# Hybrid attention and retention layer on one Trainium2 core: last gating on VectorE with its store on GpSimd's queue, retention's roots stored by one transfer, first product of attention's half 0 one step earlier

## The chip, the core and the metric

The kernel runs on one core of one Trainium2 chip. The core has a matmul engine (TensorE, PE in the profile, with its weight loads under PEld), three engines for elementwise work (VectorE = DVE, ScalarE = ACT, GpSimd = POOL) and SyncE (SP), which does nothing here but issue DMA transfers. Each engine takes its instructions in order; a transfer issued from a queue waits there until its operands are ready, and everything behind it on that queue waits with it. The metric is the device time of one execution in microseconds; less is better. Before the change three runs took 1901.03, 1903.34 and 1903.62 us, median 1903.34.

## What is computed

One layer on x of 2048 tokens by 1024 channels. The reference, cut to what matters:

```python
h = rms_norm(x, norm_gain)
q_a, k_a, v_a, g_a, q_r, k_r, v_r, g_r, m_a, m_r = split_columns(h @ w_in)
o_a = chunk_band_attention(q_a, k_a, v_a, rel_bias)      # 8 heads of 64, own chunk of 64 and 8 before
branch_a = (o_a * silu(g_a)) @ w_out_attn                # "gating" of attention
o_r = retention_chunkwise(rotary(q_r), rotary(k_r), v_r, gn_gain)   # 8 heads, keys 64, values 128
#   ... at its end: o = (o - mean) * rsqrt(var + GN_EPS), per head and token
branch_r = (o_r * silu(g_r)) @ w_out_ret
mixed = sigmoid(m_a) * branch_a + sigmoid(m_r) * branch_r
return rms_norm(x + mixed @ w_out, final_gain)
```

## The kernel before

**Dense stream.** All projections (`p0`, `g0`, `p1`, `g1`, then the two output projections `ba`, `br`, and `out`) are one long list of products of 128x128 by 128x512 tiles. Every fp32 operand is split in two parts (h and l), so that a product takes three matmuls (h by h, h by l, l by h); these three are one **dense step**, about 0.68 us of PE. Accumulators lie in PSUM (`ps_p_*`, `ps_g_*`, `ps_ba_*`), epilogues on DVE and ACT read them out, and results that a later part needs go through DRAM scratch.

**Phases.** The tokens are taken in two halves s = 0, 1. The order is proj0, attention of half 0 (att0), retention of half 0 (ret0), proj1, att1, ret1, and the merge (mrg). Dense steps are woven into the attention and retention phases by hand (`fill(n)` makes n dense steps). `later(n, fn)` emits fn n dense steps from now; `put(lag, dst, src)` is such a deferred store on SP's queue (`dma`, L154). `flush()`, at the end of a phase, emits what is still deferred. So the code itself sets the order on each engine; only in the merge may DVE, ACT and POOL be reordered by a scheduler.

**Tiles of a phase.** Each phase opens its own pool `E` of 128x512 tiles (11 buffers in attention, 12 in retention, L56 and L57). The pool of the next phase lies on the memory of the one before, and a tile waits for the last users of the memory that it lies on, so a load of the next phase may wait for a store of the phase before. In the built program the transfers of SP's and ACT's queues also share eight completion semaphores in rotation; a transfer that comes round to one still in use waits for its owner.

**Attention** (`attention`, from L1413). A unit is a head h and a block b of 512 tokens; a half has 16 units, b = 2s and 2s+1 for each head. Scores (`wide`) get bias and minimum on DVE, exponential on ACT, scaling on POOL (`pr`); PE transposes them in six groups (`tp`), ACT and DVE split each into `pth` and `ptl`, and `product` (L1547) multiplies them with the values into the PSUM tile `po`, which all units share. A group's product comes `PV_LAG` = 3 dense steps after its transposes, two more for group 0 (L1569). After group 5 `out_` (L1560) adds the two halves of `po` into `oa` (ACT copy, then DVE add), POOL multiplies `oa` by the gate `ua` three steps later, and SP stores it to DRAM scratch `oas` six steps after `out_`. The next phase begins with SP's loads of `kr` and `qr`, the keys and queries of the first retention step, for which PE waits to make the scores `sr`; POOL clears parts of `qr` first.

**Retention** (`retention`, from L1615). 4 pairs p of heads by 4 time steps of 256 tokens in each half. `sums` (L1790) adds the squares of row r = 4 (st - 4s) + p into the PSUM tile `ssq` with a one-hot weight. At the end of the phase a chain of 12 small DVE operations on 16 rows makes the inverse roots (`rt`, the tile `y`), and four stores of 8x1x256 put them into the scratch `rss`, laid out by block and head; chain and stores take one deferred step each, 16 in all, and as many dense steps go under them. The merge and the second pass read them back as `rb` (`finish_yr`, L1240).

**Behind the two retentions.** proj1 begins with four loads `b_p` of weight columns of its second chunk (L1956 and on): ACT casts them (`wh_p`), DVE forms the rests (`wl_p`, `t_p`). About the same time SP refills the resident operands `r` from scratch `cs`. The merge begins with loads of `raw_ba` (weights of `ba0`), `ga` (gates, read in by `before_ba`, used by the epilogue at L1275), `oas` and, for `finish_yr`, `yr`, `yv` and `rb`; DVE gates `yr` (L1248, L1251), ACT and DVE split it into `r` (L1257, L1258).

Of the kernel before, what the change touches and what calls it, by code (L numbers as in the profile page):

```python
# [16 lines left out]
ALU = mybir.AluOpType  # L17
# [4 lines left out]
P = 128  # L22
# [6 lines left out]
B = 512  # L29
# [31 lines left out]
PV_LAG = 3  # L61
# [12 lines left out]
def hybrid_kernel(  # L74
# [30 lines left out]
    def r32(ap):  # L105
        return ap.bitcast(F32)

    def ACC(name):
        return ps_acc.tile([P, 512], F32, tag="acc", name=name)
# [4 lines left out]
    def E(name, dt=F32, shape=(P, 512)):  # L114
        return epool[0].tile(list(shape), dt, tag="e", name=name)
# [4 lines left out]
    def D(name, shape, dt=F32):  # L120
        return dram.tile(list(shape), dt, name=name)

    def open_phase(name, e_bufs, tr_bufs=0):
        st = ExitStack()
        phase[0] = st
        epool[0] = st.enter_context(tc.tile_pool(name=f"e_{name}", bufs=e_bufs, reuse_waits="tile"))
        if tr_bufs:
            xpool[0] = st.enter_context(
                tc.tile_pool(name=f"tr_{name}", bufs=tr_bufs, space=PSUM, reuse_waits="tile")
            )  # L130
        return st
# [21 lines left out]
    pe, act, dve, pool = Ordered(nc.tensor), Sometimes(nc.scalar), Sometimes(nc.vector), Sometimes(nc.gpsimd)  # L153
    dma = Ordered(nc.sync).dma_start  # L154
# [27 lines left out]
    oascr = [[D(f"oas_{p}_{b}", [P, B]) for b in range(NB)] for p in range(4)]  # L182
# [7 lines left out]
    escr = D("escr", [HEADS, 511])  # L190
    bandscr = [D(f"band_{h}", [P, 256]) for h in range(HEADS)]
    stscr = [D(f"sts_{p}", [HD, 2 * DV]) for p in range(4)]
    rsscr = [D(f"rss_{s}", [16, B]) for s in range(2)]
    skscr = [D(f"sks_{p}", [P, 2 * DV], F32R) for p in range(4)]


# [48 lines left out]
    def later(n, fn):  # L245

        order[0] += 1
        deferred.append((steps[0] + n, order[0], fn, free[0]))
        deferred.sort(key=lambda e: e[:2])
# [8 lines left out]
    def put(lag, dst, src):  # L258

        later(lag, lambda: dma(dst, src))  # L260
# [979 lines left out]
    def finish_yr(h, b, m, lead, hold=0):  # L1240

        a, u, r = (E(f"{n}_{h}_{b}") for n in ("yr", "yv", "rb"))
        dma(a, orscr[h // 2][b][h % 2])
        dma(u, urscr[h][b])
        dma(r, rsscr[b // 2][8 * (b % 2) + h].rearrange("(o d) -> o d", o=1).broadcast_to([P, B]))

        def gated():
            dve.scalar_tensor_tensor(a, a, gn[:, h:h + 1], u, ALU.mult, ALU.mult)  # L1248

        later(lead, gated)  # L1250
        later(lead + 2, lambda: (pool if m is None else dve).tensor_tensor(a, a, r, ALU.mult))  # L1251
        if m is None:
            put(lead + 8, yrscr[h], a)
            return
        wh, wl = (w[:, h % 4, :] for w in R[m])
        at = max(lead + 5, hold - steps[0])
        later(at, lambda: act.copy(wh, a))  # L1257
        later(at + 2, lambda: dve.tensor_tensor(wl, a, r32(wh), ALU.subtract))  # L1258
# [154 lines left out]
    def attention(s, sbp, ps_wide):  # L1413
# [4 lines left out]
        units = [(h, b) for h in range(HEADS) for b in (2 * s, 2 * s + 1)]  # L1418
# [106 lines left out]
        def weighted(h, b, gr):  # L1525

            k0 = 0 if b > 0 else 4
            js = ((0, 1), (2,), (3,), (4,), (5,), (7, 6))[gr]
            tp = ACC(f"tp_{h}_{b}_{gr}")
            c, cut, parts = 0, [], []  # L1530
            for j in js:
                ts = range(max(0, j - 4), min(4, j + 1))
                cut.append((j, c, ts))
                for t in ts:
                    at = (j - max(t, k0)) * P
                    pe.transpose(tp[:, c:c + P], prs[h, b, t][:, at:at + P], ident)
                    c += P

            def part(which):
                p = E(f"pt{which}_{h}_{b}_{gr}", F32R)  # L1540
                parts.append(p)
                if which == "h":
                    act.copy(p[:, 0:c], tp[:, 0:c])
                else:
                    dve.tensor_tensor(p[:, 0:c], tp[:, 0:c], r32(parts[0][:, 0:c]), ALU.subtract)

            def product():  # L1547
                for j, at, ts in cut:
                    n = len(ts) * P
                    v4 = vts[h, b - 1 + j // 4][:, j % 4, :]  # L1550
                    for i, p in enumerate(parts):
                        pe.matmul(
                            po[:, ts[0] * P:ts[0] * P + n], v4, p[:, at:at + n],
                            start=j == (0 if b > 0 else 4) and i == 0, stop=gr == 5 and j == 6 and i == 1,
                            skip_group_check=True,
                        )
                if gr == 5:
                    later(1, out_)

            def out_():  # L1560
                oa, u = E(f"oa_{h}_{b}")[0:64], uts[h, b]
                act.copy(oa, po[64:128])
                later(1, lambda: dve.tensor_tensor(oa, po[0:64], oa, ALU.add))
                later(3, lambda: pool.tensor_tensor(oa, oa, u, ALU.mult))
                put(6, oascr[h // 2][b][64 * (h % 2):64 * (h % 2) + 64], oa)

            part("h")
            later(1, lambda: part("l"))
            later(PV_LAG + (2 if gr == 0 else 0), product)  # L1569

        def plan(b):

# [42 lines left out]
    def retention(s, ps_ret):  # L1615
# [8 lines left out]
        for n in range(3):  # L1624
            t = epool[0].tile([P, 2, 2, T], F32R, tag=f"q{n}", bufs=1, name=f"qr_{s}_{n}")
# [112 lines left out]
        def sure(here):  # L1738

            while not here():  # L1740
                emit()
# [18 lines left out]
        def evacuate(p, st, ops):  # L1760
            b, un = st // 2, st % 2
            nm = f"{p}_{st}"
            got = []

            def out_():
                oz = E(f"oz_{nm}")
                o2 = E(f"o2_{nm}")
                act.copy(oz, ops)
                act.activation(o2, ops, AF.Square)
                put(  # L1770
                    2,
                    orscr[p][b][:, :, un * T:(un + 1) * T].rearrange("i p t -> p i t"),
                    oz.rearrange("p (i t) -> p i t", i=2),
                )
                later(2, lambda: high(o2))

            def high(o2):
                got.append(E(f"o2h_{nm}", F32R))
                act.copy(got[0], o2)
                later(2, lambda: low(o2))  # L1780

            def low(o2):
                got.append(E(f"o2l_{nm}", F32R))
                pool.tensor_tensor(got[1], o2, r32(got[0]), ALU.subtract)

            later(1, out_)

            def sums():
                sure(lambda: len(got) == 2)
                r = 4 * (st - 4 * s) + p  # L1790
                for n, t in enumerate(got):
                    pe.matmul(
                        ssq, ohr[:, ONE - r:ONE - r + 16], t, start=not begun[0],
                        stop=(p == 3 and st == 4 * s + 3 and n == 1), skip_group_check=True,
                    )
                    begun[0] = True

            return sums
# [14 lines left out]
        for n, (p, st, i) in enumerate(items):  # L1813
# [24 lines left out]
        y, tmp, hv, var = (E(f"rt{n}")[0:16] for n in range(4))  # L1838
        chain = [
            lambda: dve.tensor_scalar(var, ssq, 1.0 / DV, GN_EPS, ALU.mult, ALU.add),  # L1840
            lambda: dve.tensor_scalar(tmp.bitcast(I32), var.bitcast(I32), 1, None, ALU.logical_shift_right),
            lambda: dve.tensor_scalar(y.bitcast(I32), tmp.bitcast(I32), -1.0, RSQRT_MAGIC, ALU.mult, ALU.add),
        ]
        for _ in range(3):
# [2 lines left out]
                lambda: dve.tensor_tensor(tmp, tmp, y, ALU.mult),  # L1847
                lambda: dve.scalar_tensor_tensor(y, tmp, 1.5, y, ALU.add, ALU.mult),
            ]
        dst = rsscr[s].rearrange("(b p i) (u t) -> b u p i t", b=2, p=4, u=2)  # L1850
        for n in range(4):
            chain.append(lambda n=n: dma(dst[n // 2, n % 2], y[4 * n:4 * n + 4].rearrange("p (i t) -> p i t", i=2)))
        for n, fn in enumerate(chain):
            later(1 + n, fn)
        fill(len(chain))
# [2 lines left out]
    st = open_phase("proj0", E_PROJ, 4)  # L1858
# [89 lines left out]
    st = heads(0)  # L1948
# [4 lines left out]
    st = open_phase("proj1", E_PROJ, 4)  # L1953
    ch = jobs[2].chunks[1]
    ch.b = {}
    for key in ("b11", "b12", "b21", "b22"):  # L1956
        ch.b[key] = E(f"{key}_p1", shape=(P, 4, P))
        j, h = int(key[1]) - 1, int(key[2]) - 1
        dma(ch.b[key], w_cols(w_in, jobs[2].cols[1], 2, j)[:, :, h * P:(h + 1) * P])
    run_to(end["g0"])  # L1960
    for h in range(HEADS):
        later(10 + 44 * h, lambda h=h: finish_yr(h, 0, None, 18))
# [4 lines left out]
    st = heads(1)  # L1967
# [4 lines left out]
    st = open_phase("mrg", E_MRG, 4)  # L1972

    free_at = end["br0"] - 12
    for s, (first, every, of) in enumerate((YR_0, YR_1)):
        for n, (i, h) in enumerate((i, h) for i in range(1 - s, 2) for h in range(HEADS)):
            hold = free_at + h % 4 if s and i and h > 3 else 0
            later(
                first + every * n // of,
                lambda s=s, i=i, h=h, hold=hold: finish_yr(h, 2 * s + i, RYR[s][i, h // 4], 8, hold),  # L1980
            )
# [60 lines left out]
```

## Time and profile before

| what | value |
|---|---|
| median of three runs | 1903.34 us |
| the profiled execution's own time | 1904.93 us |
| its span (first to last instruction) | 1903.1 us |
| granted TensorE clock, mean | 0.998 |
| PE busy | 1862.7 us, 98% of the span |
| PE idle, whole span | 40.4 us |
| DVE, ACT, POOL busy | 72%, 49%, 35% |
| mean DMA rate | 227 GB/s |

How to read the rows shown below. A row of the timeline has start, duration, engine, line, operation and its tiles (out<-in, buffer numbers left out), shape, how many of it stand there together, and in brackets how long the engine was idle just before and on whom it waited. Nearly every operation goes through one helper, so its line is 143, and tiles tell them apart. A row of the waits has engine, tile, releaser, then the total, the number and the longest in us. `SPq` is SP's queue of DMA issues; its duration includes what the issue waited for if several stand in one row. A row of the windows has, for each stretch, its length, the busy time and count of PE, PEld, DVE, ACT and POOL in that order, then the granted clock, the DMA share and GB/s.

### The profile page before, as it was taken

Reading aid. Unit: us, or ns where it says so; the run is one execution under the profiler, and the core shown is the slowest. Engines: PE = TensorE matmul, PEld = TensorE weight load, DVE = VectorE, ACT = ScalarE, POOL = GpSimd, SP = SyncE. Lnnn points to the kernel's source line nnn. Section 1 sums busy time; section 2 is a strip of 40 time slices with the busy share of each in tenths; the row PEclk is TensorE's granted clock in tenths of the full one; section 3 lists DMA queues with packets and bytes.
Section 4 is the critical chain, followed back from the end, with each engine's and each line's share of the span. In section 5 each row is a group of like instructions: output and inputs, shape, how many; then the busy total and the mean of one; then the engine's idle time right before and its main releaser. Section 6 shows DMA issues by size and latency. Waiting matters only on the chain. (4 is left out here: it accounts for less than half of the span.)

```text
span 1903.1 us, 30704 instructions
## 1 busy us (share of the span) xinstructions
PE 1862.7 (98%) x10149; PEld 1597.1 (84%) x10149; DVE 1364.7 (72%) x2456; ACT 933.1 (49%) x1931; POOL 671.8 (35%) x595
## 2 busy tenths in 40 slices
PE   7999999999999999999999999999999999999998
PEld 6899889888888887799889888888888878888886
DVE  6879888667655657888798677765556666767665
ACT  7555554666654555443343566664455321223544
POOL 0102106455645662001105545555564100001775
PEclk9999999999999999999999999999999999999999
DMA  6586976666549986766766646555998899987673
GB/s 195 158 281 194 281 267 219 187 183 192 175 130 271 272 244 232 243 226 206 233 236 200 197 152 196 168 151 155 254 269 293 289 355 349 332 289 223 207 237 132
DMA packets 319919, 431.58 MB, mean 227 GB/s; under 512 B 28344, under 2 KB 193808, under 8 KB 319760
## 3 DMA queue, kind: packets, MB, share of 16 engines
q1 hardware_dynamic: 254464, 364.07, 60.1%
q10 hardware_dynamic: 65296, 65.55, 11.3%
q8 instruction: 81, 1.33, 0.3%
q14 instruction: 78, 0.64, 0.1%
HBM read 283.93 MB, written 145.57 MB: 226 GB/s over the span
## 5 line engine op out<-in xcount | busy, mean ns | idle before, releaser
L143 POOL TENSOR_SCALAR pr<-pr,rsum 128x640 f32<-128x640 f32 (+4 forms) x128 | 99.8, 780 | 197.5 <-DVE rsum L143 133.7
L143 DVE TENSOR_TENSOR ptl<-tp,pth 128x512 fp32r<-128x512 f32 (+1 forms) x168 | 100.2, 597 | 95.4 <-ACT pth L143 78.2
L143 ACT ACTIVATE pr<-pr,mn 128x640 f32<-128x640 f32 (+4 forms) x128 | 97.9, 765 | 121.6 <-DVE mn L143 98.8
L143 PE MATMUL ps_g_x<-r,wh_g 128*128 128x512 f32 x448 | 141.8, 398 | 0.8 <-ACT u_g L143 0.7
L143 PE MATMUL ps_g_z<-r,wh_g 128*128 128x512 f32 x448 | 141.1, 396 | 0.0
L143 POOL TENSOR_TENSOR l_vr<-vrt,h_vr 128x512 fp32r<-128x512 f32 x32 | 47.9, 1497 | 200.0 <-DMA qrs<-l_q 131.4
L143 POOL TENSOR_TENSOR t_out<-raw_out 128x512 f32<-128x512 f32 x7 | 14.1, 2009 | 264.2 <-DVE wl_out L143 264.2
L143 DVE CUSTOM_DVE_ANT_0 pr<-wide,bt 128x640 f32<-128x640 f32 (+4 forms) x128 | 93.6, 731 | 16.7 <-PE wide L143 13.6
L143 ACT CAST pth<-tp 128x512 fp32r<-128x512 f32 (+1 forms) x168 | 85.1, 507 | 40.3 <-PE tp L143 31.3
L143 PE MATMUL wide<-ka,qa 128*128 128x384 f32 (+1 forms) x448 | 95.2, 329 | 4.0 <-DVE mn L143 3.5
L143 PEld LDWEIGHTS ps_g_x<-r,wh_g 128*128 128x128 f32 x448 | 80.4, 189 | 14.6 <-ACT u_g L143 2.0
L143 PEld LDWEIGHTS tp<-ident,pr 128*128 128x128 f32 x560 | 71.7, 140 | 24.8 <-POOL pr L143 2.4
L143 DVE TENSOR_TENSOR sm<-sr,dm 128x384 f32<-128x384 f32 x64 | 35.5, 555 | 77.2 <-PE sr L143 28.6
L143 PE MATMUL tp<-ident,pr 128*128 128x128 f32 x560 | 89.6, 273 | 1.2 <-POOL pr L143 0.9
L143 ACT CAST wh_p<-raw_p 128x512 fp32r<-128x512 f32 x111 | 68.0, 619 | 46.3 <-PE ps_p_y L143 16.3
L143 PEld LDWEIGHTS ps_g_z<-r,wh_g 128*128 128x128 f32 x448 | 79.8, 188 | 12.9
L143 PE MATMUL ps_g_x<-r,wl_g 128*128 128x512 f32 x224 | 88.4, 394 | 0.0
L143 PE MATMUL ps_g_z<-r,wl_g 128*128 128x512 f32 x224 | 88.2, 394 | 0.0
L143 POOL TENSOR_TENSOR wl_g<-t_g,wh_g 128x512 fp32r<-128x512 f32 x56 | 75.7, 1352 | 27.8 <-ACT wh_g L143 26.9
L143 DVE TENSOR_TENSOR wl_p<-raw_p,wh_p 128x512 fp32r<-128x512 f32 x111 | 79.4, 722 | 7.4 <-ACT wh_p L143 5.5
L143 POOL TENSOR_TENSOR sl<-sm,sh 128x384 fp32r<-128x384 f32 x64 | 71.9, 1124 | 35.5 <-ACT sh L143 13.7
L143 POOL TENSOR_TENSOR t_g<-raw_g,t_g 128x512 f32<-128x512 f32 x56 | 73.8, 1317 | 27.3 <-PE sr L143 4.6
(928 smaller groups left out, 6005.5 us busy)
## 6 DMA issues: line engine op xcount, KB each, us to landing
raw_g<-in_w_in_dram ACTq DMA_DIRECT2D x56, 512.0 KB, 4.2
raw_p<-in_w_in_dram ACTq DMA_DIRECT2D x50, 512.0 KB, 5.7
qa<-qas SPq DMA_DIRECT2D x128, 128.0 KB, 3.2
vr<-vrs SPq DMA_DIRECT2D x32, 512.0 KB, 7.2
ka<-kas SPq DMA_DIRECT2D x56, 256.0 KB, 4.4
va<-vas SPq DMA_DIRECT2D x40, 256.0 KB, 3.2
kds<-kdt_k SPq DMA_DIRECT2D x32, 256.0 KB, 5.8
vas<-vat SPq DMA_DIRECT2D x64, 128.0 KB, 4.2
```

The costliest lines, as they stand in the source:

```text
L143: return tc.keep_in_program_order(op(*a, **k))
```

## The change

**Last unit of attention.** For the last unit of a half, h = 7 and b = 2s + 1, the multiplication by the gate goes from POOL (three steps after `out_`) to DVE (two steps after it), and its store goes from SP's queue (six steps after) to GpSimd's (`pool.dma_start`, three steps after). The other 15 units of a half are as before.

**Retention's roots.** The scratch `rss` becomes [2, 4, 1024] for a half: head of the pair, pair, token. Row r of `ssq` becomes 4p + (st - 4s). So one store of 16x2x256 takes the place of four of 8x1x256; the chain has 13 steps, not 16, and three fewer dense steps go under it. The readers of `rb` take their slice from the new layout.

**Lag of the first group.** Group 0's product comes PV_LAG + 1 + s steps after its transposes: 4 in half 0 and 5 in half 1, where it was 5 in both.

```diff
-    rsscr = [D(f"rss_{s}", [16, B]) for s in range(2)]
+    rsscr = [D(f"rss_{s}", [2, 4, 2 * B]) for s in range(2)]
...
-        dma(r, rsscr[b // 2][8 * (b % 2) + h].rearrange("(o d) -> o d", o=1).broadcast_to([P, B]))
+        dma(r, rsscr[b // 2][h % 2, h // 2, b % 2 * B:b % 2 * B + B].rearrange("(o d) -> o d", o=1).broadcast_to([P, B]))
...
                 later(1, lambda: dve.tensor_tensor(oa, po[0:64], oa, ALU.add))
+                dst = oascr[h // 2][b][64 * (h % 2):64 * (h % 2) + 64]
+                if (h, b) == units[-1]:
+                    later(2, lambda: dve.tensor_tensor(oa, oa, u, ALU.mult))
+                    later(3, lambda: pool.dma_start(dst, oa))
+                    return
                 later(3, lambda: pool.tensor_tensor(oa, oa, u, ALU.mult))
-                put(6, oascr[h // 2][b][64 * (h % 2):64 * (h % 2) + 64], oa)
+                put(6, dst, oa)
...
-            later(PV_LAG + (2 if gr == 0 else 0), product)
+            later(PV_LAG + (1 + s if gr == 0 else 0), product)
...
-                r = 4 * (st - 4 * s) + p
+                r = 4 * p + st - 4 * s
...
-        dst = rsscr[s].rearrange("(b p i) (u t) -> b u p i t", b=2, p=4, u=2)
-        for n in range(4):
-            chain.append(lambda n=n: dma(dst[n // 2, n % 2], y[4 * n:4 * n + 4].rearrange("p (i t) -> p i t", i=2)))
+        dst = rsscr[s].rearrange("i p (s t) -> (p s) i t", s=4)
+        chain.append(lambda: dma(dst, y.rearrange("r (i t) -> r i t", i=2)))
```

**SP at the end of att0.** These are the rows of SP's queue before, from the last store of a gate result of half 0's attention (`mas`) to the loads of the first retention step; `oas_1_258<-oa_1_7044` is the last unit's store.

```order
L143 DMA mas_0_325<-g_0_1_0_6991 128x512
L143 DMA oas_1_258<-oa_1_7044 64x512
L143 DMA kr_0_7097<-krs_0_181 64x2x256 x2
L143 DMA qr_0_7088<-qrs_0_189 64x2x512
L143 DMA qr_0_7088<-qrs_0_189 64x2x256
L143 DMA dm_0_7102<-in_dmask_dram 128x384
```

In the changed kernel the same stretch of SP's queue reads:

```order
L143 DMA mas_0_325<-g_0_1_0_6991 128x512
L143 DMA kr_0_7097<-krs_0_181 64x2x256 x2
L143 DMA qr_0_7088<-qrs_0_189 64x2x512
L143 DMA qr_0_7088<-qrs_0_189 64x2x256
L143 DMA dm_0_7102<-in_dmask_dram 128x384
```

The store is gone from SP. On POOL it now stands where the multiplication stood, ahead of a `t_g` of the dense stream and the clearing of `qr`; DVE has the multiplication directly behind the addition that makes `oa`. With the new lag the buffers of the pool are taken in another order too: before, the first `kr` lay on the last `oa` and waited for its store; now the first `qr` does, and `kr` waits only for PE's last product of attention.

**PE in att0.** These are PE's rows before, around the first product of the unit h = 1, b = 1 (`po<-pth_1_0`, `ptl_1_0`); `tp_1_2` are the transposes of group 2, `wide` are scores of the next unit, `ps_g_2_w` belongs to the dense stream.

```order
L143 MATMUL ps_g_2_w<-r_84,wh_g_2_5_4738 128x512
L143 MATMUL ps_g_2_w<-r_85,wh_g_2_5_4738 128x512
L143 MATMUL ps_g_2_w<-r_84,wl_g_2_5_4739 128x512
L143 MATMUL tp_1_2_4955<-ident,pr_1_0_4772 128x128
L143 MATMUL tp_1_2_4955<-ident,pr_1_1_4801 128x128
L143 MATMUL tp_1_2_4955<-ident,pr_1_2_4834 128x128
L143 MATMUL tp_1_2_4955<-ident,pr_1_3_4872 128x128
L143 MATMUL wide<-ka_0_4839,qa_0_1_4893 128x512 x2
L143 MATMUL po<-pth_1_0_4903,va_0_4733 128x128
L143 MATMUL po<-ptl_1_0_4907,va_0_4733 128x128
L143 MATMUL po<-pth_1_0_4903,va_0_4733 128x256
L143 MATMUL po<-ptl_1_0_4907,va_0_4733 128x256
```

In the changed kernel:

```order
L143 MATMUL po<-pth_1_0_4903,va_0_4733 128x128
L143 MATMUL po<-ptl_1_0_4907,va_0_4733 128x128
L143 MATMUL po<-pth_1_0_4903,va_0_4733 128x256
L143 MATMUL po<-ptl_1_0_4907,va_0_4733 128x256
L143 MATMUL ps_g_2_w<-r_84,wh_g_2_5_4738 128x512
L143 MATMUL ps_g_2_w<-r_85,wh_g_2_5_4738 128x512
L143 MATMUL ps_g_2_w<-r_84,wl_g_2_5_4739 128x512
L143 MATMUL tp_1_2_4959<-ident,pr_1_0_4772 128x128
L143 MATMUL tp_1_2_4959<-ident,pr_1_1_4801 128x128
L143 MATMUL tp_1_2_4959<-ident,pr_1_2_4834 128x128
L143 MATMUL tp_1_2_4959<-ident,pr_1_3_4872 128x128
L143 MATMUL wide<-ka_0_4839,qa_0_1_4893 128x512 x2
```

The four matmuls of group 0's product have moved ahead of one dense step, the transposes of group 2 and the scores behind them; the same is so for the seven other units with b = 1, and in half 1 nothing of it moves.

**SP from ret0 to proj1.** SP's rows before, from a refill of `r` to the next stores of the dense stream (`mrs`); `rt` is the tile with the roots, `b_p` are the weights of proj1's second chunk.

```order
L143 DMA r_89<-cs_98 128x512 x4
L143 DMA rss_430<-rt_9029 8x1x256
L143 DMA mrs_0_373<-g_0_3_0_9069 128x512
L143 DMA rss_430<-rt_9029 8x1x256
L143 DMA r_91<-cs_99 128x512 x4
L143 DMA rss_430<-rt_9029 8x1x256 x2
L143 DMA b_p_9165<-in_w_in_dram 128x4x128
L143 DMA b_p_9167<-in_w_in_dram 128x4x128
L143 DMA b_p_9169<-in_w_in_dram 128x4x128
L143 DMA b_p_9171<-in_w_in_dram 128x4x128
L143 DMA r_87<-cs_97 128x512 x4
```

In the changed kernel:

```order
L143 DMA r_89<-cs_98 128x512 x4
L143 DMA rss_430<-rt_9029 16x2x256
L143 DMA mrs_0_373<-g_0_3_0_9069 128x512
L143 DMA b_p_9140<-in_w_in_dram 128x4x128
L143 DMA b_p_9142<-in_w_in_dram 128x4x128
L143 DMA b_p_9144<-in_w_in_dram 128x4x128
L143 DMA b_p_9146<-in_w_in_dram 128x4x128
L143 DMA r_91<-cs_99 128x512 x4
L143 DMA r_87<-cs_97 128x512 x4
```

The four `b_p` now come ahead of the refill `r_91<-cs_99` and have one `rss` store before them where there were four. At the same place behind ret1, the load of `raw_ba` and a `ga` now stand ahead of the single `rss` store, and `yr`, `yv`, `rb` come three dense steps sooner.

## Prediction

> **What bounds the kernel now.** I read the page's busy times first, then PE's waits, then the timeline around each wait.
>
> ```profile
> span 1903.1 us, 30704 instructions
> PE 1862.7 (98%) x10149; PEld 1597.1 (84%) x10149; DVE 1364.7 (72%) x2456; ACT 933.1 (49%) x1931; POOL 671.8 (35%) x595
> ```
>
> PE works 1862.7 of 1903.1 us, and the change takes no matmul away. All that it can win lies in PE's 40.4 us of idle time, or in matmuls that run at a lower clock. PE's waits, largest first and those that the change reaches in the merge:
>
> ```profile
> PE gains L143 <- DMA gains<-in_norm_gain_dram: 9.2, 1, 9.2
> ...
> PE ps_ba_(0, 0)_18423 L143 <- DVE ga L1275: 0.9, 1, 0.9
> PE ps_ba_(1, 0)_18375 L143 <- DVE ga L1275: 0.5, 1, 0.5
> PE ps_ba_(0, 1)_18249 L143 <- DVE ga L1275: 0.5, 1, 0.5
> PE ps_ba_(1, 1)_18198 L143 <- DVE ga L1275: 0.4, 1, 0.4
> PE ps_ba_(0, 1)_18444 L143 <- DVE ga L1275: 0.2, 1, 0.2
> ```
>
> The 9.2 us are the start and stay. The rest is a scatter of waits of 0.2 to 1.8 us, so a gain has to be found one wait at a time, at the places that the change touches. I cost it place by place, against the profiled run's own 1904.93 us, 1.83 above its span. That run is 1.59 above the median of the three; the sum is carried over to the median.
>
> **Step 1, att0 to ret0.** SP, POOL, DVE and PE there:
>
> ```profile
> 559.19 0.68 DVE L143 TENSOR_TENSOR oa<-po,oa 64x512 f32<-64x512 f32 x1
> 559.95 1.28 POOL L143 TENSOR_TENSOR oa<-oa,ua 64x512 f32<-64x512 f32 x1 [5.49 <-DVE oa L143]
> 561.22 0.69 DVE L143 TENSOR_TENSOR c_g<-ps_g_z,u_g 128x512 f32<-128x512 f32 x1 [1.35 <-PE ps_g_z L143]
> 561.25 0.46 SPq L143 DMA_DIRECT2D oas<-oa  x1
> 561.83 1.20 DVE L143 TENSOR_TENSOR wl_g<-raw_g,wh_g 128x512 fp32r<-128x512 f32 x1
> 563.60 1.30 SPq L143 DMA_DIRECT2D kr<-krs  x2
> 565.32 1.22 SPq L143 DMA_DIRECT2D qr<-qrs  x2
> 568.66 1.29 POOL L143 TENSOR_TENSOR wl_g<-t_g,wh_g 128x512 fp32r<-128x512 f32 x1 [4.56 <-ACT wh_g L143]
> 573.11 0.65 PE L143 MATMUL sr<-qr,kr 128*128 128x256 f32 x4 [1.72 <-DMA qr<-qrs]
> ```
>
> Now: the last `oa` is gated on POOL until 561.23, stored at 561.25, and the store holds up `kr` until 563.60, so it lands about 2.3 us after its issue; `qr` goes at 565.32, and PE waits 1.72 us for it. After: DVE's addition ends at 559.87, the multiplication follows (about 0.7 us, as the addition), in the 1.35 us in which DVE waited before `c_g`, so it delays nothing. The store is issued near 560.6. `kr` waits only for PE's last `po`, so it goes first; `qr` waits for the store. If GpSimd's store lands as SP's did, 560.6 + 2.3 = 562.9; I allow 564. Then `qr` goes 1.3 to 2.4 us sooner, and most or all of 1.72 goes. On POOL the store is ahead of `t_g` and the clearing of `qr`; the idle 4.56 us before `wl_g` covers up to that much of lateness there.
>
> Behind this wait stands a second loss, the granted clock (column before the DMA share):
>
> ```profile
> 574.00:576.00 2.00, 2.00 (x9) 1.71 (x8) 1.34 (x3) 1.03 (x2) 0.00 (x0) 0.50 1.08 230
> 576.00:578.00 2.00, 2.00 (x8) 1.58 (x7) 0.77 (x2) 0.51 (x1) 1.57 (x2) 0.68 1.07 289
> ```
>
> At 0.50 and 0.68 PE does 1.00 and 1.36 us of full-speed work in 4 us, so 1.64 us are lost. I take it that the wait set this off: both go, 1.72 + 1.64 = 3.36 at most; I take **-3.0**, since some tenths may stay. Upper end: past 563.6 each us that the store lands later takes back a us of the wait, and at 565.3 nothing is won: 0.
>
> The Trainium skill ("TensorE: Matmul & The Clock Gate", Part 1) says that the half clock comes from a window of about 3.4 us seen idle, and asks for no PE-idle gaps beyond about 3 us. The half clock agrees with 0.50 here; by its length 1.72 us should not have set it off. Two rows bear on that rule:
>
> ```profile
> 277.54 1.20 PE L143 MATMUL pst<-ident,xs 128*128 128x128 f32 x4 [1.83 <-ACT xs L143]
> ```
>
> ```profile
> 278.00:280.00 2.00, 2.00 (x15) 1.73 (x15) 0.51 (x1) 2.00 (x8) 0.00 (x0) 1.00 0.97 328
> ```
>
> A gap of 1.83 us kept the clock at 1.00. So a gap of this size does not always lower it, and the drop may stand there for a reason of its own; then step 1 brings only -1.4. That is a rival below.
>
> **Step 2, group 0 one step sooner in att0.**
>
> ```profile
> 362.98 0.66 DVE L143 TENSOR_TENSOR oa<-po,oa 64x512 f32<-64x512 f32 x1
> 365.07 0.22 PE L143 MATMUL po<-pth,va 128*128 128x128 f32 x1
> 389.50 0.62 PE L143 MATMUL ps_g_w<-r,wh_g 128*128 128x512 f32 x2
> 391.46 0.22 PE L143 MATMUL po<-pth,va 128*128 128x128 f32 x1
> 393.01 0.59 ACT L143 CAST pth<-tp 128x512 fp32r<-128x512 f32 x1 [1.60 <-POOL oa L143]
> 394.98 0.50 PE L143 MATMUL wide<-ka,qa 128*128 128x256 f32 x2 [0.73 <-DVE mn L143]
> 500.63 0.50 PE L143 MATMUL wide<-ka,qa 128*128 128x256 f32 x2 [0.75 <-DVE mn L143]
> ```
>
> The four matmuls of group 0's product move ahead of a dense step, four transposes and two scores, which in head 1 take from 389.50 to 391.46, 1.96 us. Its `pth` comes free sooner, so group 2's `pth` in the heads 1 and 5 takes that buffer, not one that waits for POOL's gating: ACT's wait of 1.60 goes, the DVE work behind it moves up, and the waits 0.73 and 0.75 go: -1.48. Against it, `po` is written sooner, and must wait for the previous unit's `oa` to be read: for head 0 that read ends at 362.98 + 0.66 = 363.64, and the product, now at 365.07, would start at 363.11: +0.5. Other heads come close to the same, without being counted. Net **-0.9**, bounds -1.5 and +0.6. In att1 the lag stays 5: nothing.
>
> **Step 3, ret0 to proj1.**
>
> ```profile
> 742.43 0.66 SPq L143 DMA_DIRECT2D rss<-rt  x1
> 743.20 1.89 SPq L143 DMA_DIRECT2D r<-cs  x4
> 746.48 4.40 SPq L143 DMA_DIRECT2D b_p<-in_w_in_dram  x4
> 749.99 0.62 ACT L143 CAST wh_p<-b_p 128x512 fp32r<-128x512 f32 x1 [2.46 <-PE ps_g_z L143]
> 751.67 0.73 PE L143 MATMUL ps_p_x<-r,wh_p 128*128 128x512 f32 x2 [1.54 <-ACT u_p L143]
> 758.26 0.50 PE L143 MATMUL ps_p_y<-r,wl_p 128*128 128x512 f32 x1 [0.41 <-DVE wl_p L143]
> ```
>
> Now, by the order of the queue, four `rss` stores and a refill `r` stand ahead of `b_p`. ACT casts the first `b_p` only at 749.99, behind it comes ACT's `u_p`, and for that PE waits 1.54. After, `b_p` is issued about where the second `rss` stood, 742.4, so 4.1 us sooner than 746.48, and the cast is no longer late; the refill behind it has slack that no row shows exactly. The 1.54 goes, and 0.41 probably: **-2.0**. Bounds: -3.0 (with two later waits on the same split work) and 0, if `r` becomes the late one.
>
> **Step 4, ret1 to merge.**
>
> ```profile
> 1502.41 0.39 SPq L143 DMA_DIRECT2D raw_ba<-in_w_out_attn_dram  x1
> 1505.26 0.38 SPq L143 DMA_DIRECT2D yr<-ors  x1
> ```
>
> ```profile
> 1500.00:1550.00 50.00, 47.49 (x205) 37.82 (x204) 34.95 (x55) 12.59 (x21) 0.00 (x0) 1.00 0.94 338
> ```
>
> `raw_ba` no longer stands behind a root store that waits for DVE's chain, and moves up by some us; `yr` comes three dense steps sooner, about 2 us. PE's five waits on `ga` above are 0.9 + 0.5 + 0.5 + 0.4 + 0.2 = 2.5 us. They end with DVE, which takes `yr` and `ga` in an order and gets both from DMA. But the DMA share is 0.94 in this stretch: a transfer that goes first makes another later. I take **-1.5**, bounds -2.5 and +1.0.
>
> **Step 5, att1 to ret1.** The same edit as step 1 works here:
>
> ```profile
> 1314.98 1.22 SPq L143 DMA_DIRECT2D qr<-qrs  x2
> 1330.54 0.48 PE L143 MATMUL o<-qr,sstk 128*128 128x256 f32 x2 [0.69 <-DMA sstk<-sks]
> ```
>
> `qr` was not late for PE here; `sstk` was, by 0.69. With one transfer fewer on SP's queue the rotation of completion semaphores shifts, and `sstk` comes behind another owner. I take **+0.3**, bounds -1.0 and +1.5.
>
> Sum: -3.0 - 0.9 - 2.0 - 1.5 + 0.3 = -7.1; 1904.93 - 7.1 = 1897.8 for a run like the profiled one, and 1903.34 - 7.1 = **1896.2** as a median. The ends do not all come together; root sums of the distances give about -2 and +5, so 1894 to 1901.
>
> **The rivals.**
>
> *The clock drop stays* (the rule above as a mechanism). Only the wait goes: 1896.2 + 1.6 = 1897.8. For it: 277.54. Against: the drop begins right behind 573.11. Chance 0.15.
>
> *The store lands late, at about 565.* Step 1 brings nothing: 1896.2 + 3.0 = 1899.2. For it: this trace has no store from GpSimd's queue at all. Against: SP's took 2.3. Chance 0.15.
>
> *The waits move on.* Steps 3 and 4 bring transfers ahead of others while DMA runs at 0.94; what is passed (`r`, `ga`) is late instead, and with step 5 at +1.5 only step 1 and half of step 2 are left (-3.4), against +1.5 in step 5 and 0.5 of new waits: -1.4, so 1901.9. The shift of the semaphore rotation through all later phases speaks for it. Chance 0.18.
>
> *GpSimd's store is held up by DVE* (slower). DVE runs `c_g` and the 1.20 us `wl_g` from 561.22 on, then further two-input operations. If the store can go out only in DVE's longer idle time, it lands after 568, and `qr` waits for it. In ret0 each us beyond 565.3 is a us of PE; in ret1 `qr` went at 1314.98, and the slack is unknown, bounded by 0. With 5 us in each place, and the clock drop, that is 10 us against the -4.1 of the steps 2 to 5: 1903.34 + 5.9 = 1909.2. It decides as soon as both together pass 8 us. Against it: DVE is idle between those operations. Chance 0.10. [...]
>
> That the change does less than its words is settled by the order of the instructions: the lag moves only half 0, and is counted so.
>
> **How the numbers follow.** The forecast has 0.42, the first two rivals 0.15 each: all three are faster by over 0.2%, which is 3.8 us and about what a measurement of this kernel can tell from no change. So faster 0.42 + 0.15 + 0.15 = 0.72, same 0.18, slower 0.10. The range leaves out the slower case and ends that need all good bounds: 1891.5 to 1903.5, which takes in the third rival.
>
> **What would show it.** Right: the timeline after has PE's `sr` of ret0 without a wait for `qr` and granted clock 1.00 behind it; no wait for `u_p` at proj1's start; the waits on `ga` under 1 us in sum; none of `wide` for heads 1 and 5. Wrong: a store on GpSimd's queue that lands more than 4 us after its issue; `sr` still waiting; new waits for `r` in proj1 or on DMA in the merge that take back what the first steps brought; in ret1, `sstk` or `vr` later by over a us.

## The result, and the profile after

The changed kernel took 1894.68 us, median of six runs (1893.96 to 1896.64), against 1903.55 (six runs, 1901.03 to 1906.46) of the kernel before: a ratio of 0.995, 95% interval 0.994 to 0.9961, 8.9 us faster. A second series on another occasion, six runs against eleven of the kernel before, gave 0.9947 (0.9935 to 0.996). The forecast was 7.1 us.

The page after, its first lines, and PE's waits:

```profile
span 1892.8 us, 30703 instructions
...
PE 1858.8 (98%) x10149; PEld 1597.0 (84%) x10149; DVE 1364.5 (72%) x2458; ACT 933.8 (49%) x1931; POOL 671.3 (35%) x595
```

```profile
PE kv L143 <- DMA vr<-vrs: 2.2, 2, 1.2
PE wide L143 <- DVE mn L143: 2.0, 3, 1.1
...
PE o L143 <- DMA sstk<-sks: 1.1, 1, 1.1
...
PE ps_ba_(1, 0)_18465 L143 <- DVE ga L1275: 0.7, 1, 0.7
```

In the profile before, the row of `wide` was:

```profile
PE wide L143 <- DVE mn L143: 3.5, 5, 1.1
```

The wait for `qr` and the wait for `u_p` are gone from the list, `wide` has three waits where it had five, and of five waits on `ga` one is left. At the top now stands `kv`, which waits for `vr`, the values of a retention step. One of its two waits was there before (1.66, in ret1); the other one, of 0.93 in ret0, is new.

Att0 to ret0, the engines after:

```profile
556.81 1.27 SPq L143 DMA_DIRECT2D kr<-krs  x2
558.27 0.68 DVE L143 TENSOR_TENSOR oa<-oa,ua 64x512 f32<-64x512 f32 x1
559.26 0.73 POOL L143 DMA_DIRECT2D oas<-oa  x1 [6.33 <-DVE oa L143]
560.03 1.31 POOL L143 TENSOR_TENSOR t_g<-raw_g,raw_g 128x512 f32<-128x512 f32 x1
560.20 1.69 DVE L143 TENSOR_TENSOR wl_g<-raw_g,wh_g 128x512 fp32r<-128x512 f32 x1
561.80 1.22 SPq L143 DMA_DIRECT2D qr<-qrs  x2
569.61 0.57 PE L143 MATMUL sr<-qr,kr 128*128 128x256 f32 x4
583.37 0.71 PE L143 MATMUL kv<-vr,kd 128*128 128x256 f32 x4 [0.93 <-DMA vr<-vrs]
```

```profile
574.00:578.00 4.00, 4.00 (x26) 3.56 (x25) 2.25 (x5) 1.74 (x4) 2.93 (x3) 1.00 1.09 321
```

`kr` goes before the store, `qr` 2.54 us behind the store's start, `sr` starts without a wait, and the clock is 1.00. Then, 14 us later, PE waits 0.93 for `vr`: what was late next.

Ret0 to proj1, PE before and after at the wait for `u_p`; first before:

```profile
749.73 0.39 PE L143 MATMUL ps_g_z<-r,wl_g 128*128 128x512 f32 x1
751.67 0.73 PE L143 MATMUL ps_p_x<-r,wh_p 128*128 128x512 f32 x2 [1.54 <-ACT u_p L143]
752.23 0.40 PE L143 MATMUL ps_p_x<-r,wl_p 128*128 128x512 f32 x1
...
776.22 0.50 PE L143 MATMUL ps_p_z<-r,wl_p 128*128 128x512 f32 x1 [0.56 <-DVE wl_p L143]
```

And after, with the load that decides it:

```profile
738.65 2.50 SPq L143 DMA_DIRECT2D b_p<-in_w_in_dram  x4
746.66 0.39 PE L143 MATMUL ps_g_z<-r,wl_g 128*128 128x512 f32 x1
746.88 0.61 PE L143 MATMUL ps_p_x<-r,wh_p 128*128 128x512 f32 x2
747.34 0.39 PE L143 MATMUL ps_p_x<-r,wl_p 128*128 128x512 f32 x1
```

These rows show a cost that the bracket doesn't hold. Without a wait the three starts are 0.22 and 0.46 apart. With it they are 1.94 and 0.56 apart: 1.82 more, for a wait of 1.54. The matmuls overlap, so a wait also costs the overlap, and the first pair behind it runs slower (0.73 for 0.61). This wait costs **0.28 us more than its bracket**; I call that its restart.

I then set each matmul's start after against its start before, along the whole program. The difference grows in steps, and the steps are what each place gave in this pair of profiles:

| place | forecast | measured | shift at its end |
|---|---|---|---|
| start and proj0 | 0 | +0.57 | +0.57 |
| att0 | -0.9 | -2.29 | -1.72 |
| att0 to ret0 | -3.0 | -2.37 | -4.09 |
| rest of ret0 | 0 | +1.01 | -3.08 |
| ret0 to proj1 | -2.0 | -4.20 | -7.28 |
| rest of proj1, att1 | 0 | -0.08 | -7.36 |
| att1 to ret1 | +0.3 | -0.05 | -7.41 |
| merge | -1.5 | -2.89 | -10.30 |

Around six single waits that went (two in att0, four in proj1) the shift grows by 0.20 to 0.37 more than the bracket, so 0.28 is a fair middle. About 1.7 of the 10.30 are the low clock of the one execution before (3.41 us at 0.50); without it the pair differs by 8.6, near the 8.9 of the medians.

### The profile page after: what moved, and what is told of

Same layout as the page of the kernel before. It is cut to its first block, busy times and chain, and to the rows that moved or that the text cites. A ratio compares the mean times of both kernels' runs of the same rounds, so it can differ in the third digit from the quotient of the medians.

```text
span 1892.8 us, 30703 instructions
## 1 busy us (share of the span) xinstructions
PE 1858.8 (98%) x10149; PEld 1597.0 (84%) x10149; DVE 1364.5 (72%) x2458; ACT 933.8 (49%) x1931; POOL 671.3 (35%) x595
```

## Experiments

Every ratio is against runs of the kernel before on the same chip, with its 95% interval.

**The three parts alone.** The lag alone:

```diff
-            later(PV_LAG + (2 if gr == 0 else 0), product)
+            later(PV_LAG + (1 + s if gr == 0 else 0), product)
```

> The lag change alone. Theory: it does two things. In att0 the waits 0.73 and 0.75 of PE on the minimum go, each with some tenths of restart, -2.3 as between the two profiles. And because the buffers are taken in another order, the first kr of ret0 no longer waits for the last store of att0, only qr does, so qr goes at about 563.7 instead of 565.3, and PE's wait of 1.72 mostly goes, though gating is still on POOL and the store on SP: -1.5 to -3. Together 1898 to 1900. Rival (the gating on DVE and the store on GpSimd's queue bring step 1): only att0's part is seen, PE still waits about 1.7 for qr with the low clock behind it: about 1901.3.

Ratio 0.9969 (0.9957 to 0.9981), 5.9 us. SP and PE at the start of ret0:

```profile
558.38 0.46 SPq L143 DMA_DIRECT2D oas<-oa  x1
558.94 1.29 SPq L143 DMA_DIRECT2D kr<-krs  x2
...
568.36 0.57 PE L143 MATMUL sr<-qr,kr 128*128 128x256 f32 x4
```

Gated on POOL and stored from SP as before, `kr` goes 0.10 us behind the store's issue and `sr` doesn't wait. The theory holds.

The roots alone (the edits at `rsscr`, `finish_yr`, `sums` and the chain):

```diff
...
-        for n in range(4):
-            chain.append(lambda n=n: dma(dst[n // 2, n % 2], y[4 * n:4 * n + 4].rearrange("p (i t) -> p i t", i=2)))
+        chain.append(lambda: dma(dst, y.rearrange("r (i t) -> r i t", i=2)))
```

> The single store of the roots alone. Theory: the waits at proj1's start go (0.41 to 1.54 each with about 0.3 of restart, -4.1 between the two profiles) and most of those on ga in the merge (-2.9): 1897 to 1898. Rival: the merge's share came from the shifted rotation of completion semaphores, not from the store, and is not seen here: about 1899.5, with the waits on ga still 2 us or more in sum.

Ratio 0.9964 (0.9952 to 0.9976), 6.9 us. Proj1 behaves as in the changed kernel. In the merge it doesn't:

```profile
PE ps_ba_(0, 0)_18418 L143 <- DVE ga L1275: 1.0, 1, 1.0
...
PE ps_ba_(1, 0)_18465 L143 <- DVE ga L1275: 1.0, 1, 1.0
...
PE ps_ba_(0, 1)_18439 L143 <- DVE ga L1275: 0.3, 1, 0.3
```

2.3 us of waits on `ga` with the new queue order: as the rival had it. The time fits the theory better, the rows the rival; the merge is taken up below.

The last unit's gating and store alone:

```diff
...
+                if (h, b) == units[-1]:
+                    later(2, lambda: dve.tensor_tensor(oa, oa, u, ALU.mult))
+                    later(3, lambda: pool.dma_start(dst, oa))
+                    return
...
```

> The gating of the last unit on DVE and its store on GpSimd's queue alone. Theory: with the old lag the first kr of ret0 still lies on the last oa and waits for the store to land, at about 563.0 instead of 563.6, so qr is only 0.6 sooner, PE still waits about 1.1 for it, and the low clock behind it may stay: 1902 to 1903. Rival (this part carries step 1 by itself): PE's wait for qr and the low clock go, 1900 to 1900.5.

Ratio 0.9993 (0.9983 to 1.0003): no difference that can be told.

```profile
561.95 0.68 DVE L143 TENSOR_TENSOR oa<-oa,ua 64x512 f32<-64x512 f32 x1
562.94 0.73 POOL L143 DMA_DIRECT2D oas<-oa  x1 [6.47 <-DVE oa L143]
565.51 1.27 SPq L143 DMA_DIRECT2D kr<-krs  x2
574.05 0.65 PE L143 MATMUL sr<-qr,kr 128*128 128x256 f32 x4 [0.67 <-DMA qr<-qrs]
```

DVE is done at 562.63, the transfer starts 0.31 later and frees `kr` 2.57 after that: most of what DVE saves against POOL goes into the other queue.

The same with the store on SP (`put(3, dst, oa)` in place of the third line):

> As the run before, but the store stays on SP's queue (three steps after out_ instead of six). Theory: the store lands about 2.3 us after its issue from either queue, and kr waits for the landing either way, so the queue decides nothing here: within 1 us of the run with GpSimd's queue, PE's wait for qr about 1.1. Rival: what counts is that nothing stands ahead of kr on SP: then this run has the full wait of 1.7 and the other does not, and it is 1.5 us or more slower than the other.

Ratio 0.9994 (0.9982 to 1.0006).

```profile
561.48 0.46 SPq L143 DMA_DIRECT2D oas<-oa  x1
563.82 1.29 SPq L143 DMA_DIRECT2D kr<-krs  x2
573.01 0.65 PE L143 MATMUL sr<-qr,kr 128*128 128x256 f32 x4 [0.76 <-DMA qr<-qrs]
```

2.34 us from the issue to `kr`, and about the same wait of PE: the queue decides nothing that can be told, as the theory had it. In both runs the wait is under the 1.1 that was expected.

**The changed kernel with one thing taken back.** First itself once more, for a second profile on the same chip as the three runs behind it.

> The changed kernel once more, with a second profile, next to the three runs that follow. Theory: its waits belong to the program: no wait for qr in ret0, none for u_p in proj1, one wait of about 0.7 on ga in the merge, and 0.5% less time than before; the low clock belongs to the execution and may show at any wait of over 1.4 us. Rival: the merge's waits belong to the execution too (a busy DMA), then their sum differs from 0.66 by over 1 us.

Ratio 0.9947 (0.9935 to 0.996). No wait for `qr`, none for `u_p`, none for `vr` in ret0 this time, and in the merge two waits on `ga`:

```profile
1535.27 0.73 PE L143 MATMUL ps_ba_(0, 1)_18439<-r,wh_ba_(0, 0)_18346 128*128 128x512 f32 x2 [0.39 <-DVE ga L1275]
1539.33 0.70 PE L143 MATMUL ps_ba_(1, 0)_18465<-r,wh_ba_(1, 0)_18387 128*128 128x512 f32 x2 [1.04 <-DVE ga L1275]
```

1.43 in sum against 0.66: less than the 1 us that the rival asked for, but executions of one program differ here by most of what is in question.

Its store on SP's queue:

> The changed kernel with the last unit's store on SP's queue (still at the third step, still gated on DVE). Theory: the store comes near 559 and lands 2.3 us later from either queue, qr waits for that, kr goes at about 559.5 instead of 556.8 and still in time: no wait for qr, within 1 us of the changed kernel. Rival: the empty place on SP's queue is worth something: 1.5 to 3 us slower than the changed kernel.

Ratio 0.9937 (0.9925 to 0.9949): not slower, and PE has no wait for `qr`. The rival falls.

The whole first part taken back (POOL gates, SP stores at the sixth step; lag and roots stay):

> The changed kernel without its first part: gated on POOL, stored from SP at the sixth step. Theory: the lag's order of buffers alone lets kr go ahead of the store's landing, as in the run with the lag alone, which had no wait for qr: within 1 us of the changed kernel, and no wait for qr. Rival: the first part is worth what it did alone, 1.3 us: 1 to 2 us slower than the changed kernel with a wait for qr of some tenths.

Ratio 0.9937 (0.9924 to 0.995).

```profile
561.14 0.46 SPq L143 DMA_DIRECT2D oas<-oa  x1
561.70 1.30 SPq L143 DMA_DIRECT2D kr<-krs  x2
...
571.12 0.57 PE L143 MATMUL sr<-qr,kr 128*128 128x256 f32 x4
```

No wait for `qr`, and no slower than the full change. Lag and roots account for the whole gain as far as these runs can tell: 5.9 and 6.9 alone, 12.0 together, with intervals of 2.3 to 2.5 us on each side.

One root store, but 16 steps:

```diff
+        chain += [lambda: None] * 3
```

> The changed kernel with one root store but 16 steps, the last three empty. Theory: what wins is the place on SP's queue. In proj1 three stores are gone but the refill r stands ahead of b_p again, so b_p goes about 1.4 us sooner than before, and the wait for u_p is 0 to 0.3 where it was 1.54; in the merge raw_ba stands behind the root store again, and the waits on ga are 1.5 to 2.5 in sum: 1.5 to 3.5 us slower than the changed kernel. Rival: the number of stores decides, not the steps: within 1 us of the changed kernel.

Ratio 0.9949 (0.9938 to 0.9961), level with the changed kernel's 0.9947: the rival's result.

```profile
739.39 2.07 SPq L143 DMA_DIRECT2D b_p<-in_w_in_dram  x4
745.87 0.73 PE L143 MATMUL ps_p_x<-r,wh_p 128*128 128x512 f32 x2 [0.25 <-ACT u_p L143]
```

In proj1 the theory was right (0.25 of wait came back); in the merge the waits were 1.94 in sum, inside what it expected, but 0.5 above the second profile of the changed kernel, and the time shows no loss. By the time, the number of stores decides, and the steps show nothing.

**The kernel before, a second profile.**

> The kernel before, a second profile. Theory: the 1.72 us wait for qr and the low clock behind it belonged to that one execution; in the runs that kept the old order of kr and qr the wait was 0.5 to 0.8 and the clock was 1.00 there, so here the wait is 0.5 to 0.9 with no low clock at 574, while u_p (about 1.5) and the two waits of about 0.74 on the minimum are the program's and come again. Rival: 1.72 is the program's own; 1.5 or more here too.

```profile
565.56 1.22 SPq L143 DMA_DIRECT2D qr<-qrs  x2
573.08 0.65 PE L143 MATMUL sr<-qr,kr 128*128 128x256 f32 x4 [1.46 <-DMA qr<-qrs]
...
751.16 0.73 PE L143 MATMUL ps_p_x<-r,wh_p 128*128 128x512 f32 x2 [2.15 <-ACT u_p L143]
```

My theory fell: the wait for `qr` is 1.46, just under the rival's 1.5, and belongs to the program. Its size varies: in the five profiles with `kr` behind the store's landing it was 0.53 to 1.72, and the 0.53 came with the gating on POOL (the roots alone), so the shorter waits with the gating on DVE say nothing for DVE. Only the low clock belonged to the one execution: here the clock is 1.00 behind the wait. The waits on `ga` sum to 2.51, as in the first profile.

**Is it the buffers or the earlier product?** The kernel before with the lag at 5, and the gate tile `ua` in two buffers of its own:

```diff
-E_ATT = 11
+E_ATT = 9
...
-            uts[h, b] = E(f"ua_{h}_{b}")[0:64]
+            uts[h, b] = sbp.tile([P, 512], F32, tag="ua", bufs=2, name=f"ua_{h}_{b}")[0:64]
```

> The kernel before with the lag left at 5, but the gate tile ua in two buffers of its own and nine instead of eleven in the pool: the same memory. Theory: the lag wins by the order of the buffers and not by PE's earlier product; here group 2's pth of the heads 1 and 5 no longer takes a buffer that the gating on POOL holds, and kr and qr of ret0 no longer wait for the last store to land, so the two waits of 0.74 and the one for qr go as with the lag alone: a ratio near 0.997 (3 to 7 us faster than before). Rival: the earlier product itself wins: the waits of 0.74 stay and the time is within 1.5 us of before.

Ratio 1.0207 (1.0193 to 1.0221): 39 us slower, and no answer to the question.

```profile
404.11 0.56 DVE L143 TENSOR_TENSOR ptl<-tp,pth 128x384 fp32r<-128x384 f32 x1 [6.26 <-DMA oas<-oa]
```

```profile
404.93 1.22 PE L143 MATMUL wide<-ka,qa 128*128 128x512 f32 x2 [6.44 <-DVE mn L143]
```

```profile
404.00:406.00 2.00, 1.07 (x3) 0.89 (x4) 1.37 (x4) 0.50 (x2) 0.00 (x0) 0.50 0.00 0
```

With nine buffers in the ring a `ptl` waits for the store of an `oa` that is still due; DVE stands 6.26 us, and PE behind it 6.44. That happens six times (3.87 to 6.67 us), and each brings a stretch at half clock, 6.83 us long in five cases and 3.41 in one. The same memory and the same lag: how the buffers are shared out is worth tens of us by itself, but whether their order or the earlier product took the two waits of 0.74 away is not shown.

**The lag of 4 in both halves** (`PV_LAG + (1 if gr == 0 else 0)`).

> The changed kernel with the lag of 4 in both halves. Theory: att1 has one wait of 0.46 on the minimum and two of 0.25 and 0.7 on POOL's scaling, none of which hangs on group 0's buffer, so nothing is won there; behind att1 the first kr now waits for the last store instead of qr: 0 to 2 us slower than the changed kernel. Rival: one step less is worth as much in half 1 as in half 0: 2 to 4 us faster.

Ratio 0.9965 (0.9952 to 0.9977), by the ratios about 3 us behind the changed kernel; the ends of the intervals just overlap. One of six places in att1:

```profile
1214.33 0.68 DVE L143 TENSOR_TENSOR oa<-po,oa 64x512 f32<-64x512 f32 x1
```

```profile
1215.06 0.33 PE L143 MATMUL po<-pth,va 128*128 128x128 f32 x1 [0.44 <-DVE oa L143]
```

The product overtakes DVE's reading of `po`, and PE waits 0.29 to 0.44, six times: 2.12 in sum, and a restart each. That is the price that step 2 put on half 0 (0.5 for head 0); half 0 shows no such wait, half 1 does. The theory was too mild and missed a part: PE's two waits on POOL's scaling (0.71 and 0.25) did go. Against the first profile of the changed kernel, att1 takes 3.7 us more; the waits for `sstk` and `vr` in ret1 are gone too, and 1.9 us come back there.

**Loads of the second retention step sooner**, in the changed kernel (the loop behind these lines then leaves out the load that has already been made):

```diff
+        load_state(*todo[0])
         load_scored(*todo[1])
-        load_state(*todo[0])
+        load_valued(*todo[1])
...
```

> The changed kernel, with the loads of the state and its split form ahead of the second step's keys at the start of ret1, and the second step's values (kd, vr) ahead of the stores of the gates, in both retentions. Theory: of the waits that are left in the changed kernel, those for sstk (0 to 1.1) and for vr (1.1 to 1.2, in ret0 0 to 0.9) come from SP's queue, which stands for 4 to 7 us behind a weight load that owns its next semaphore; ahead of that they go, with 0.3 of restart each: 1.5 to 3.5 us faster than the changed kernel. Rival: DMA is the bound there, and the loads land no sooner, or kr and qr take their place: within 1 us, with a wait of the same size for another tile.

Ratio 0.9938 (0.9925 to 0.995), against 0.995 and 0.9947 for the changed kernel: 1 to 2 us, inside the intervals.

```profile
1320.99 0.65 PE L143 MATMUL sr<-qr,kr 128*128 128x256 f32 x4 [0.71 <-issue]
...
1330.54 0.65 PE L143 MATMUL sr<-qr,kr 128*128 128x256 f32 x4 [0.57 <-DMA qr<-qrs]
```

The waits for `sstk` and `vr` are gone and two waits for the next scores stand in their place: both accounts hold in part (for the first of the two the profile shows no releaser). It is not shown to beat the changed kernel.

## Why the prediction was right

**What bounds it.** Right: PE's matmuls are unchanged, and what was won are waits, their restarts and the one stretch of low clock. PE's idle time fell by 6.4 us and its busy time by 3.9, in which the low clock and the slower pairs behind waits are gone.

**Step 1 (-3.0, measured -2.4).** The wait went as forecast: `kr` ahead of the store, no wait, clock 1.00. `qr` goes 3.5 us sooner in the profile; 1.7 of that PE had already gained before, so `qr` gained 1.8 on PE, within the 1.3 to 2.4 of the forecast. Three points of the step were off.

First, the step worked its time out from the multiplication on DVE and the early store. The runs show no gain from these (0.9993 alone, and nothing lost without them); the lag, which lets `kr` go ahead of the store's landing, is enough by itself. Second, the question "what is late next" I left open, and it was `vr`: 0.93 and its restart came back. Third, the low clock was counted as a sure effect of the wait, though the wait of 1.83 at 277.54 had none. Stretches of 3.41 us in the profile before show what parts the two:

```profile
273.51:276.92 3.41, 2.20 (x19) 2.00 (x17) 3.38 (x6) 0.00 (x0) 0.00 (x0) 1.00 1.06 325
570.47:573.88 3.41, 1.69 (x11) 1.17 (x10) 0.09 (x1) 0.02 (x1) 2.11 (x2) 1.00 1.07 291
573.88:577.29 3.41, 3.41 (x12) 2.83 (x11) 2.23 (x4) 1.52 (x3) 0.86 (x1) 0.50 1.08 245
```

In each profile the granted clock changed only at the lines of one grid of 3.41 us. The wait of 1.72 lay whole in one stretch of it, and the next stretch ran at 0.50. The wait of 1.83 was parted by the line at 276.92 into 1.21 and 0.62, and the clock stayed at 1.00. I counted PE's idle time by such stretches, from the first stretch at 1.00 to the last matmul in all fourteen profiles: each stretch at full clock with 1.72 us or more idle was followed by one at half clock, none with 1.47 or less was, and of six with 1.53 to 1.65 three were. So the same wait costs 1.7 us more or nothing, by where the execution lays it on the grid. The first rival was half right: that clock was no sure gain, but it had no reason of its own either. How often it fell in the runs of the median is not on record.

The Trainium skill ("TensorE: Matmul & The Clock Gate", Part 1) calls the window of about 3.4 us free-running, so that the place of a gap in it matters beside its length: this agrees with the grid of 3.41, and with a gap of 1.53 doing what one of 2.42 (1.37 and 1.05 by stretches) did not. Its rule in the same part, "no PE-idle gaps >~3.4µs", names gaps that did lower the clock here each time (3.87 and more), but it does not cover the drops behind gaps of 1.53 to 2.17.

**Step 2 (-0.9, measured -2.3).** The two waits went, each with a restart of 0.2, and the counter-term of +0.5 for `po` did not come in half 0.

**Step 3 (-2.0, measured -4.2).** All four waits up to 776.22 went, 1.54 + 0.41 + 0.39 + 0.56 = 2.90, plus four restarts: 2.90 + 4 x 0.28 = 4.0. The term was mis-sized: I counted two of the waits (the other two stood in its bound of -3.0), and none of the restarts. The refill `r` behind `b_p` did not become late.

**Step 4 (-1.5, measured -2.9).** `raw_ba` did move up, from 1502.41 to 1488.21, of which 7.4 are the shift so far, and the waits fell from 2.51 to 0.66, four fewer, with restarts 1.85 + 1.1 = 3.0. But executions scatter: over eight profiles with the single store the waits on `ga` sum to 0.66 to 2.31, 1.50 in the mean, over five with four stores and the old pool (two of before, one with the lag alone, two with the last unit alone) to 1.74 to 2.67, 2.31 in the mean. So some 0.8 us of waits go with the single store, and the rest of this pair's gain is scatter. The sign that was set for it, under 1 us of waits on `ga`, held in the first profile of the changed kernel (0.66) and not in the second (1.43). What sets these waits from one execution to the next stays open; a DMA that works at 0.94 there is a guess that fits.

**Step 5 (+0.3, measured 0.0).** `sstk` became later (1.09 for 0.69) and `vr` earlier (1.23 for 1.66), within the bounds.

**The rivals.** *The store lands late*: no, 2.54 us. *GpSimd's store is held up by DVE*: no. In att0 DVE ran the two-input `wl_g` right behind the store's issue, and `qr` went 2.54 us after it (2.57 for `kr` with the last unit alone), where a store of SP's took 2.34. In att1 such a `wl_g` ran during the issue itself, and `qr` went after 2.38:

```profile
1304.90 0.58 POOL L143 DMA_DIRECT2D oas<-oa  x1 [3.63 <-DVE oa L143]
1305.29 0.68 DVE L143 TENSOR_TENSOR wl_g<-raw_g,wh_g 128x512 fp32r<-128x512 f32 x1
1307.28 1.23 SPq L143 DMA_DIRECT2D qr<-qrs  x2
```

The Trainium skill ("SBUF — State Buffer", the "DVE blocks DMA" trap) warns of a DVE operation in a 2-port mode beside such a store; it does not name operations with two SBUF inputs, which are what the rival was built on. *The waits move on*: in part, 0.93 for `vr` and 1.01 in the rest of ret0, where POOL's splits come late for PE (waits of 0.52 and 1.03 where one of 0.30 stood), not the 5.7 us (from -7.1 to -1.4) that it needed.

That the sum came out near is in part luck, as errors of both signs met: against the forecast, +0.6 at the start, +0.6 in step 1 and +1.0 behind it; -1.4, -2.2 and -1.4 in the steps 2 to 4, mostly restarts and waits not counted; -0.4 in step 5 and the stretch before it. That makes -3.2 between the two profiles. The low clock of 1.7 belongs to the one profiled execution and not to every run of the median; without it half of that gap closes again.

## What to carry to other kernels

Cost a wait on a pipelined engine at its bracket plus a restart, here 0.2 to 0.4 us, and count every wait down the chain that the moved load feeds, not only the first. Where a pool's buffers are taken in rotation, an edit that shifts the order of allocation can decide who waits for whom at the next phase; look up the tile that a load lies on before giving the credit to the engine or the queue that was changed. Count a drop of the clock as a chance, not as a part of the wait. And test the parts alone: of the three edits here two account for the gain, and the one that the first step was credited to showed none of its own.

## What the runs showed of the hardware

Counted from its start on POOL, a store from GpSimd's queue freed its reader after 2.51 to 2.57 us behind att0 and after 2.38 to 2.47 behind att1; one from SP's queue took 2.34 to 2.37 behind att0, wherever a load waited for it. Behind att0 the first kind also started 0.31 us after DVE's multiplication, the second 0.03 after it. The 128x512 `wl_g` of DVE took 1.69 and 1.74 us while POOL ran `t_g` on two SBUF inputs beside it, where it takes 0.68 alone. The granted clock changed only on a grid of 3.41 us, and 1.53 us of idle PE inside one stretch of it was the least that was followed by half clock.
